# A state-space stage with its channel scales spread first, B and C loaded on two queues, and the first gate panel's units placed between the last read-outs

## The chip, the cores and the metric

One core of a Trainium2 chip runs the whole program. The time is device microseconds of one execution; each kernel is run several times and the median is given. One further execution is taken by the hardware profiler, and all rows of the trace are from that one. The engines are TensorE (PE, its weight loads PEld), VectorE (DVE), ScalarE (ACT), GpSimd (POOL), and SyncE (SP), which issues most transfers.

## The reference

A decoder trunk of two layers over x of 256 steps by 2048 channels, all in float32. A vector c gives six modulation rows per layer (shift, scale and gate for the mixer and for the FFN) by a product with ada_w. Layer 0 mixes with a diagonal state-space model, layer 1 with a convolution; each mixer is followed by a SwiGLU FFN and each sub-layer ends in a LayerNorm. Of layer 0's mixer:

```python
mod = c_act @ ada_w[i] + ada_b[i]            # (2048) x (2048, 6 * 2048), c_act = silu(c)
h = x * (1.0 + sc_m) + sh_m
a_bar = exp(lam * dt)                        # 128 groups of 16 channels, 64 complex states each
b_bar = ((a_bar - 1) / lam) * B              # B: (128, 64, 16) complex, C: (128, 16, 64) complex
state[t] = a_bar * state[t-1] + b_bar @ u[t] # u = h, by groups
y = gelu(real(C @ state) + d_skip * u)
vg = y @ w_glu                               # (256, 2048) x (2048, 4096)
out = vg[:, :2048] * sigmoid(vg[:, 2048:])
```

## The kernel before

**Loads.** A weight "unit" is 512 rows by 512 columns of float32, 1 MB. The modulation of layer 0 is built on PE: 56 units of ada_w (14 blocks of four units, `ada_block`, line 600 on) are multiplied by c_act (line 610), the block's sum is copied to `adas` (ACT, 613), turned (`adat`, 617) and reduced on DVE (`adasum`, 619; `mod`, 620). `ada_units(n)` takes the next n units. They arrive in the `raw` buffers, four at first and six in the loop, all issued by SP in program order, so a load waits for a buffer and everything behind it on SP waits too.

**Preparation.** lam and log_dt are loaded first and turned, and DVE computes exponentials, sines and tables from them (`prep`, lines 67 to 73 of the helper). `load_mats` (210) loads the real and imaginary halves of B and C, C in pieces of 256 bytes so that the two groups of a pair lie together. `turn_mats` (231) turns them on PE (line 240), ACT copies them out (`cm`, 243). `matrices` and `quarter` build the products (`mu`, `qb`, `qc`, line 313) and power tables (`tq`, 351) of four tiles at a time, on DVE for the first four tiles and on POOL for the rest.

**The loop.** 16 tiles of 128 channels. For tile ct: `weights` makes its matrices on ACT and PE (`mb`, `btr`, `lz`; `mc`, `dd`, `bdp`, `bd`); `tables` doubles the table once more (DVE for tile 0, POOL after); `inputs` turns x (`xt`), and ACT scales it with the modulation (`uh`, line 922). The scales have to lie in the states' layout for that: `half_mod` spreads four tiles' scales and shifts with two products (`hmod`, 1268). `drive` gives the states' input (`pin`, 418); `scan` is DVE's recurrence over two half sequences (`x`, `pin`, `pc`, `psn`, lines 435 to 460); `read_out` is the product with C (`y`, 484); `gelu` (1296 to 1306) makes hh and hl, the high and low parts of the next product's input. In turn ct of the loop stand weights, one unit, tables of tile ct+1, the read-out of tile ct-1, inputs, a unit, drive of ct+1, a unit, and then the scan of ct with the gelu of ct-1 between its steps. PE's order is the program's here; the other engines' is the scheduler's, and a call under `queue_behind` or `issue_after` is placed behind the instruction named.

**The gate panels.** w_glu is taken in 8 panels of 512 columns, each of four units, by `gemm` (line 819). For each unit ACT makes `whi` (811) and DVE `wlo` (812), two buffers of each; PE does 24 products (861). The sums `acc` come from a pool of four banks that is opened when the banks of `pin` are given up, so after scan 15. `before` calls `s5_end`, tile 15's read-out and gelu, ahead of unit 2. From panel 1 on an ada queue adds 1.05 steps per unit: a 1 MB load `rawa`, and DVE's sums `adaacc` (678, 680).

Of the kernel before, what the change touches and what calls it, by code (L numbers as in the profile page):

```python
# [153 lines left out]
class S5:  # L154
# [76 lines left out]
    def turn_mats(self):  # L231
        nc, cm = self.nc, self.cm

        for q, n in enumerate(self.nat):
            src = n.rearrange("p (a i) -> p a i", i=GI) if q == 0 else n.rearrange("p (i a) -> p i a", i=GI)
            for h in range(4):
                b = self.bank("turn")
                for i in range(4):
                    one = src[:, :, 4 * h + i] if q == 0 else src[:, 4 * h + i]
                    nc.tensor.transpose(b[:, i * P:(i + 1) * P], one, self.ident)  # L240
# [131 lines left out]
    def weights(self, ct, skip):  # L372

        nc = self.nc
        dd = self.dd[ct % 3]
# [8 lines left out]
        for par in range(2):  # L384
            ps = slice(64 * par, 64 * par + 64)
            nc.scalar.copy(out=mc[ps, 0:4, :, par], in_=qc[ps, :, 4 * k:4 * k + 4])
            nc.scalar.activation(out=mc[ps, 4:6, :, par], in_=qc[ps, 0:3:2, 4 * k:4 * k + 4], func=AF.Copy, scale=-1.0)
# [33 lines left out]
    def scan(self, ct, pin, tab, between):  # L421
# [10 lines left out]
        def turn(out, k):  # L432
            for a in range(2):
                o, i = (z[:, a].rearrange("p s r h c -> p (s r) h c") for z in (out, pin))
                v.tensor_tensor(out=o, in0=i, in1=bc(t[:, k, a::2], 1, 4), op=MUL)  # L435
# [55 lines left out]
def kernel(  # L491
# [311 lines left out]
    class Unit:  # L803


        def __init__(self, wp, wsrc, k0, kn, segs, behind=()):
# [3 lines left out]
            with queue_behind(behind):  # L810
# [450 lines left out]
    def half_mod(q):  # L1261
# [7 lines left out]
        nc.scalar.copy(out=hmod[:, :, :, s4], in_=b[:, 0:16].rearrange("p (h j k) -> p h j k", h=2, j=2))  # L1269

    def inputs(ct):
# [19 lines left out]
    def gelu(ct, u, y):  # L1291
# [10 lines left out]
        def third():  # L1302
            g = w.tile([P, SEQ], F32, tag="gl", name="gl", bufs=1)
            nc.vector.tensor_tensor(out=g.rearrange("p (t c) -> p t c", t=2), in0=uu, in1=vv, op=MUL)
            nc.scalar.copy(out=hh[:, ct], in_=g)
            nc.gpsimd.tensor_tensor(out=hl[:, ct], in0=g, in1=hh[:, ct].bitcast(F32), op=SUB)

# [8 lines left out]
    def start_dense():  # L1316
# [3 lines left out]
        for u in range(2):  # L1320
            ready.append(Unit(wp, s5_w_glu[0], 4 * u, 4, [(0, 256), (D, 256)]))

    const2 = wp = ln_col = wtap = fold32 = row_of = None
    with tc.manual_schedule(engines={mybir.EngineType.PE}):
        ada_units(3)
        for ct in range(-1, NCH):
            now, y = coming, None
# [21 lines left out]
            def between():
                if turns:  # L1350
                    turns.pop(0)()

            if 0 <= ct < NCH:
                held = ct, now[1], *s5.scan(ct, now[2], tabs.pop(ct), between)
                if ct % 4 == 3 and ct < 11:
# [249 lines left out]
```

## Time and profile before

| what | us |
| --- | --- |
| median of 3 runs | 2380.3 (2378.76 to 2382.05) |
| the profiled execution | 2377.07 |
| its span | 2375.3 |
| PE busy | 2276.3 (96% of the span) |
| DVE busy | 1647.3 |
| ACT busy | 1024.6 |
| start of tile 0's scan | 59.57 |
| end of tile 15's scan | 248.90 |

All positions are microseconds from the span's start. A row of the timeline gives start, duration, engine, line of the kernel before, operation, output and inputs, shapes and count, and in square brackets how long the engine stood idle before it and what released it. A row of the windows gives the stretch, its length, the busy time of each engine in it, the granted clock of PE, the busy share of the 16 DMA engines (somewhat over 1 when full) and GB/s. The state-space stage, its preparation included, is the first 250 us; the gate panels end near 440 us, and the rest is FFN, convolution and the second layer, which the change leaves as it is.

### The profile page before, as it was taken

How to read it: one execution, taken by the hardware profiler on the slowest of the kernel's cores; microseconds unless marked ns; L12 is line 12 of the kernel's file. 1: busy time of each engine (PE TensorE's matmuls, PEld its weight loads, DVE VectorE, ACT ScalarE, POOL GpSimd, SP SyncE). 2: the span in 40 equal slices, each digit the busy share in tenths (PEclk: the TensorE clock that was granted, in tenths of full speed). 3: DMA queues.
4: the chain of work that ended last, by engine and by line, in shares of the span. 5: the costliest groups of instructions: out<-in, count | busy, mean ns of one | idle time of the engine just before them, and what ended most of it. 6: DMA issues, size and time to landing. Idle time of an engine off the chain costs nothing.

```text
span 2375.3 us, 34394 instructions
## 1 busy us (share of the span) xinstructions
PE 2276.3 (96%) x14061; PEld 1818.2 (77%) x14061; DVE 1647.3 (69%) x1818; ACT 1024.6 (43%) x1267; POOL 235.3 (10%) x290
## 2 busy tenths in 40 slices
PE   5887899999999999999999999899999999999998
PEld 2444777978888888888886667688888888888888
DVE  6899788887777777777885564788655544554564
ACT  4676234564333333334463332557343333333443
POOL 2564000110000000000031111402000000000000
PEclk7998899999999999999999999999999999999999
DMA  9986599578888888888745553674775555555542
GB/s 309 353 306 207 201 325 344 186 270 304 312 300 314 308 316 297 315 305 316 269 143 177 196 195 125 241 271 161 272 243 178 195 191 181 194 183 191 185 161 98
DMA packets 373332, 572.17 MB, mean 241 GB/s; under 512 B 17171, under 2 KB 267331, under 8 KB 358579
## 3 DMA queue, kind: packets, MB, share of 16 engines
q1 hardware_dynamic: 372742, 569.53, 69.6%
q8 instruction: 110, 1.80, 0.3%
q0 software_dynamic: 192, 0.37, 0.1%
q14 instruction: 48, 0.39, 0.0%
q10 hardware_dynamic: 240, 0.08, 0.0%
HBM read 567.83 MB, written 2.10 MB: 240 GB/s over the span
## 4 chain that ended last, share of the span: by engine, by line
PE 79%; DVE 8%; issue 6%; POOL 4%; ACT 2%; DMA 1%; SPq 0%; DVEq 0%; POOLq 0%; ACTq 0%
PE acc L861 68%; PE acc L865 4%; PE conv L1501 2%; PE turned L877 2%; PE spread L1491 1%; POOL h L959 1%; DVE pin L447 1%; DVE wlo L812 1%; ACT whi L811 1%; DVE pin L435 1%; DVE pc L435 1%; DMA raw<-in_s_w_glu_dram 1%; DVE psn L435 1%; DVE x L435 0%; POOL hf L1540 0%
## 5 line engine op out<-in xcount | busy, mean ns | idle before, releaser
L812 DVE TENSOR_TENSOR wlo<-raw,whi 128x2048 fp32r<-128x2048 f32 x344 | 791.3, 2301 | 544.3 <-ACT whi L811 544.2
L811 ACT CAST whi<-raw 128x2048 fp32r<-128x2048 f32 x344 | 655.0, 1904 | 828.0 <-PE acc L861 613.5
L861 PE MATMUL acc<-whi,h 128*128 128x512 f32 x3648 | 899.4, 396 | 15.6 <-ACT whi L811 8.5
L861 PEld LDWEIGHTS acc<-whi,h 128*128 128x128 f32 x3648 | 680.1, 189 | 175.7 <-issue 17.7
L861 PE MATMUL acc<-wlo,h 128*128 128x512 f32 x1824 | 464.2, 392 | 1.0 <-DVE wlo L812 1.0
L861 PEld LDWEIGHTS acc<-wlo,h 128*128 128x128 f32 x1824 | 342.4, 188 | 77.0 <-DVE wlo L812 1.6
L861 PE MATMUL acc<-whi,f 128*128 128x512 f32 x1248 | 300.5, 391 | 0.0
L680 DVE SCALAR_TENSOR_TENSOR adaacc<-rawa,c_act,adaacc 128x2048 f32<-128x2048 f32 (+1 forms) x135 | 284.7, 2109 | 1.4 <-DMA rawa<-in_ada_w_dram 1.1
L861 PEld LDWEIGHTS acc<-whi,f 128*128 128x128 f32 x1248 | 233.0, 188 | 48.9 <-ACT whi L811 0.8
L861 PE MATMUL acc<-wlo,f 128*128 128x512 f32 x624 | 156.4, 389 | 0.0
L861 PEld LDWEIGHTS acc<-wlo,f 128*128 128x128 f32 x624 | 117.2, 188 | 24.3
L1480 POOL TENSOR_TENSOR lw<-fold,wtap 128x1024 f32<-128x1024 f32 x16 | 41.5, 2601 | 894.2 <-PE acc L865 710.2
L610 PE MATMUL ada<-raw,c_rep 128*32 128x512 f32 x512 | 75.4, 677 | 11.5 <-DMA raw<-in_ada_w_dram 6.7
L959 POOL TENSOR_TENSOR h<-hf,h 128x512 fp32r<-128x512 f32 x24 | 48.2, 2019 | 331.9 <-ACT h L958 324.7
L1184 ACT ACTIVATE fsg<-acc 128x256 f32<-128x256 f32 x84 | 31.9, 380 | 104.3 <-PE acc L861 104.3
L1130 POOL CAST lnmh<-lno 128x2 fp32r<-128x2 f32 x1 | 0.2, 182 | 713.6 <-DVE lno L65 713.6
L865 PEld LDWEIGHTS acc<-h,whi 128*128 128x128 f32 x512 | 63.3, 194 | 9.1 <-DVE h L1530 2.3
L865 PE MATMUL acc<-h,whi 128*128 128x256 f32 x512 | 67.2, 287 | 2.6 <-DVE h L1530 1.4
L1501 PE MATMUL conv<-vs,lw 128*32 128x256 f32 x1024 | 61.4, 381 | 0.4 <-DVE vs L1495 0.4
L1501 PEld LDWEIGHTS conv<-vs,lw 128*32 128x32 f32 x1024 | 33.0, 110 | 25.6 <-issue 4.5
L1185 DVE TENSOR_TENSOR fsg<-acc,fsg 128x256 f32<-128x256 f32 x84 | 35.3, 420 | 19.6 <-ACT fsg L1184 19.5
L447 DVE TENSOR_TENSOR_SCAN pin<-rho,pin 128x256 f32<-128x256 f32 x64 | 44.3, 692 | 1.6
(334 smaller groups left out, 1895.2 us busy)
## 6 DMA issues: line engine op xcount, KB each, us to landing
raw<-in_ffn_w_gu_dram SPq DMA_DIRECT2D x352, 512.0 KB, 4.4
rawa<-in_ada_w_dram SPq DMA_DIRECT2D x128, 1024.0 KB, 5.3
raw<-in_ffn_w_down_dram SPq DMA_DIRECT2D x88, 1024.0 KB, 5.0
raw<-in_ada_w_dram SPq DMA_DIRECT2D x64, 1024.0 KB, 7.4
raw<-in_s_w_glu_dram SPq DMA_DIRECT2D x64, 512.0 KB, 5.4
raw<-in_cv_w_pw_dram SPq DMA_DIRECT2D x64, 512.0 KB, 4.8
raw<-in_cv_w_pw_dram SPq DMA_DIRECT2D x16, 1024.0 KB, 5.7
X<-in_x_dram SPq DMA_DIRECT2D x8, 256.0 KB, 11.0
```

The costliest lines, as they stand in the source:

```text
L435: v.tensor_tensor(out=o, in0=i, in1=bc(t[:, k, a::2], 1, 4), op=MUL)
L447: v.tensor_tensor_scan(out=z, data0=rh[:, a].rearrange("p r h c -> p (r h c)"), data1=z, initial=0.0, op0=MUL, op1=ADD)
L610: nc.tensor.matmul(acc[32 * k:32 * k + 32, :], c_rep[:, 4 * u + k, :], r[:, k, :], start=u == 0, stop=u == 3)
L680: nc.vector.scalar_tensor_tensor(out=acc, in0=r[:, i], scalar=c_act[:, kk:kk + 1], in1=acc, op0=MUL, op1=ADD)
L811: m1 = nc.scalar.copy(out=self.hi[:, :kn], in_=r[:, :kn])
L812: m2 = nc.vector.tensor_tensor(out=self.lo[:, :kn], in0=r[:, :kn], in1=self.hi[:, :kn].bitcast(F32), op=SUB)
L861: nc.tensor.matmul(acc[bank].rearrange("p a b -> p (a b)"), x[:, bank * HALF:(bank + 1) * HALF], wt[:, k], start=first, stop=end)
L865: nc.tensor.matmul(acc[bank][:, i], wt[:, k, m * P:(m + 1) * P], x, start=first and i == 0, stop=end and i == 1)
L877: nc.tensor.transpose(b[:, o:o + HALF], u[t][:, c0 + k * P:c0 + (k + 1) * P], ident)
L959: nc.gpsimd.tensor_tensor(out=hl[:, s2], in0=h, in1=hh[:, s2].bitcast(F32), op=SUB)
L1480: nc.gpsimd.tensor_tensor(out=lw, in0=fold32.unsqueeze(1).unsqueeze(1).broadcast_to([P, 4, CONV_G, 32]), in1=bc(wtap[:, :, 4 * ch:4 * ch + ...
L1501: nc.tensor.matmul(acc[32 * q:32 * q + 32, :], lw[:, q, g, :], vs[:, q, 4 * g:4 * g + SEQ], start=g == 0, stop=g == CONV_G - 1)
```

## The change

1. `load_mats` makes four contiguous loads of 512 KB instead of two and four; the real halves are issued by SP, the imaginary halves by ACT, as ACT's first and third transfers. C then lies with the pair's groups apart, and `turn_mats` turns it with two products of 64 columns in place of one transpose.
2. `half_mod(0)`, the spreading of the first four tiles' scales, stands ahead of the loop and no longer in `inputs(0)`. The three units ahead of the loop are gone, every turn has three units, the last one too.
3. `weights` is cut in two. `weights_in` (mb, btr, lz) stays where it was; `weights_out` (dd, mc, bdp, bd) comes after `drive`. Its copies of mc are placed behind the first hmod copy. Units follow each of weights_in, inputs and weights_out.
4. The loop ends one turn sooner. Only one unit of w_glu is made ready ahead. The first gate panel gets its sums in one bank of the pool `aux` (three banks, used for y, adat, xt and others) and in the bank of `ada`; `before` becomes a table: ahead of unit 1 `last_scan` (read-out 14 and scan 15), ahead of unit 2 a mark, ahead of unit 3 `s5_end`. Unit 3 of that panel is taken by its four row blocks in turn instead of by banks.
5. `held_back`: from unit 3's casts on, whi and wlo are placed behind scan 15's last instruction, and after `s5_end` the casts and the ada steps of panel 0's rest and of panel 1 behind tile 15's gelu.

```diff
     def load_mats(self, b_re, b_im, c_re, c_im):
         nc = self.nc
-        for r, t in enumerate((b_re, b_im)):
-            nc.sync.dma_start(self.nat[0][64 * r:64 * r + 64], t.rearrange("(j a) n i -> j (a n i)", a=2))
-        for r, t in enumerate((c_re, c_im)):
-            for a in range(2):
-                nc.sync.dma_start(
-                    self.nat[1][64 * r:64 * r + 64].rearrange("p (i a n) -> p i a n", i=GI, a=2)[:, :, a],
-                    t.rearrange("(j a) i n -> j a i n", a=2)[:, a])
+        for q, parts in enumerate(((b_re, b_im), (c_re, c_im))):
+            for r, (t, eng) in enumerate(zip(parts, (nc.sync, nc.scalar))):
+                eng.dma_start(self.nat[q][64 * r:64 * r + 64], t.rearrange("(j a) x y -> j (a x y)", a=2))
...
-                    one = src[:, :, 4 * h + i] if q == 0 else src[:, 4 * h + i]
-                    nc.tensor.transpose(b[:, i * P:(i + 1) * P], one, self.ident)
+                    for a in range(2):
+                        nc.tensor.matmul(b[64 * a:64 * a + 64, k], src[:, a, 4 * h + i], self.ident, start=True, stop=True)
...
+    def weights_out(self, ct, skip, behind):
+        nc.scalar.mul(dd, self.ident, skip)
+        with self.tc.issue_after(behind.ins):
...
-            with queue_behind(behind):
+            with queue_behind([*behind, *held_back]):
                 m1 = nc.scalar.copy(out=self.hi[:, :kn], in_=r[:, :kn])
...
-            if u == 2 and before:
-                before()
-            for part in ((0,), (1,)) if last else ((0, 1),):
+            if u in before:
+                before[u]()
+            for part in ((0,), (1,)) if last and not in_turn else ((0, 1),):
...
+                if last and in_turn:
+                    order.sort(key=lambda o: o[1])
...
-        for u in range(2):
-            ready.append(Unit(wp, s5_w_glu[0], 4 * u, 4, [(0, 256), (D, 256)]))
+        ready.append(Unit(wp, s5_w_glu[0], 0, 4, [(0, 256), (D, 256)]))
...
-        ada_units(3)
-        for ct in range(-1, NCH):
+        first_mod = half_mod(0)
+        for ct in range(-1, NCH - 1):
...
+            s5.weights_in(ct + 1)
+            ada_units(1)
...
+            u, uh = inputs(ct + 1)
+            ada_units(1)
+            coming = ct + 1, u, s5.drive(ct + 1, uh)
+            s5.weights_out(ct + 1, d_col[:, ct + 1:ct + 2], first_mod)
+            ada_units(1)
...
+    def last_scan():
+        ada_turn()
+        scan(NCH - 1, coming, s5.read_out(*held))
+        pin_ctx.close()
+        accp = ctx.enter_context(tc.tile_pool(name="acc", bufs=4, space=PSUM))
...
+        first = {"acc": [b.rearrange("p (a b) -> p a b", b=SEQ) for b in (aux("acc"), bank)], "before": {1: last_scan, 2: lambda: held_back.append(s5.end), 3: s5_end}}
```

PE around tile 0, from the last units ahead of the loop to the first pin. Before (ada is one unit for every four products; adat is a block's turn, hmod the spread scales):

```order
L610 MATMUL ada<-raw,c_rep 32x512 x12
L393 MATMUL btr<-ident,mb_478 128x128 x4
L396 MATMUL bdp<-fold,dd_488 128x32
L400 MATMUL bdp<-mc_480,mb_478 32x32 x8
L610 MATMUL ada<-raw,c_rep 32x512 x4
L1276 MATMUL xt<-ident,X 128x128 x2
L1280 MATMUL xt<-ident,X 32x128 x8
L617 MATMUL adat<-ident,adas 128x128 x4
L1268 MATMUL hmod<-mod_128,sel 128x8 x2
L610 MATMUL ada<-raw,c_rep 32x512 x4
L418 MATMUL pin<-uh,lz_483 128x2x64 x8
```

The same place now, where the first row is units 6 to 8 of the program (another twelve products that stood ahead of the piece shown before):

```order
L615 MATMUL ada<-raw,c_rep 32x512 x12
L622 MATMUL adat<-ident,adas 128x128 x4
L1276 MATMUL hmod<-mod_128,sel 128x8 x2
L386 MATMUL btr<-ident,mb_492 128x128 x4
L615 MATMUL ada<-raw,c_rep 32x512 x4
L1284 MATMUL xt<-ident,X 128x128 x2
L1288 MATMUL xt<-ident,X 32x128 x8
L615 MATMUL ada<-raw,c_rep 32x512 x4
L423 MATMUL pin<-uh,lz_497 128x2x64 x8
```

Three units fewer stand ahead of pin (10 instead of 13), hmod ahead of the tile's own products, and bdp behind pin.

PE at the end of the stage, from tile 15's pin on. Before (y are the read-outs of tile 14 and then of tile 15, acc the first gate panel, 24 products a unit):

```order
L418 MATMUL pin<-uh,lz_484 128x2x64 x8
L473 MATMUL y<-u,bd_487 128x129
L474 MATMUL y<-u,dd_490 128x128
L484 MATMUL y<-pc,mc_482 32x128 x16
L484 MATMUL y<-psn,mc_482 32x128 x16
L861 MATMUL acc<-whi,h 128x512 x16
L861 MATMUL acc<-wlo,h 128x512 x8
L861 MATMUL acc<-whi,h 128x512 x16
L861 MATMUL acc<-wlo,h 128x512 x8
L473 MATMUL y<-u,bd_485 128x129
```

Now, from the last unit of ada on (bd_501 is tile 14's, bd_499 tile 15's):

```order
L615 MATMUL ada<-raw,c_rep 32x512 x4
L870 MATMUL acc<-whi,h 128x512 x16
L870 MATMUL acc<-wlo,h 128x512 x8
L622 MATMUL adat<-ident,adas 128x128 x4
L478 MATMUL y<-u,bd_501 128x129
L479 MATMUL y<-u,dd_504 128x128
L489 MATMUL y<-pc,mc_496 32x128 x16
L489 MATMUL y<-psn,mc_496 32x128 x16
L870 MATMUL acc<-whi,h 128x512 x16
L870 MATMUL acc<-wlo,h 128x512 x8
L870 MATMUL acc<-whi,h 128x512 x16
L870 MATMUL acc<-wlo,h 128x512 x8
```

Unit 0 stands ahead of read-out 14, units 1 and 2 between the read-outs, and unit 3 behind tile 15's, where units 0 and 1 stood between them and 2 and 3 behind.

DVE where scans 14 and 15 overlap (tab_2826 and tab_2792 are tile 14's, tab_2969 and tab_2950 tile 15's). Before:

```order
L812 TENSOR_TENSOR wlo<-raw,whi 128x2048
L454 TENSOR_TENSOR cx<-pin,rw 128x8
L455 TENSOR_TENSOR cy<-pin,rw 128x8
L812 TENSOR_TENSOR wlo<-raw,whi 128x2048
L457 TENSOR_TENSOR cx<-cx,cy 128x2x2
L458 TENSOR_TENSOR cx<-cx,cy 128x2x2
L435 TENSOR_TENSOR x_3128<-pin,tab_2969 128x512
```

Now:

```order
L817 TENSOR_TENSOR wlo<-raw,whi 128x2048
L440 TENSOR_TENSOR pc<-pin,tab_2792 128x512 x2
L440 TENSOR_TENSOR psn<-pin,tab_2792 128x512 x2
L817 TENSOR_TENSOR wlo<-raw,whi 128x2048
L624 TENSOR_REDUCE adasum<-adat 128x4
L440 TENSOR_TENSOR pin<-pin,tab_2950 128x512
L625 SCALAR_TENSOR_TENSOR mod_128<-adasum,adab_120 128x4
L817 TENSOR_TENSOR wlo<-raw,whi 128x2048
L440 TENSOR_TENSOR pin<-pin,tab_2950 128x512
```

Three wlo instead of two stand ahead of scan 15's main part, the last two behind scan 14's end; the two adaacc that stood within scan 15 are behind tile 15's gelu.

On ACT, ahead of tile 0's uh, there stand now two tab copies, an activation and a copy of mc; on POOL the loads of ln_g and ln_b, which wait for PE's vec_t, have moved ahead of the clears of mb, mc, bd and rho; on ACT near the end whi of units 3 and 4 stand ahead of the gelu of tile 15.

More of the change, by code (lines that the diff above doesn't have):

```diff
@@ L394, in weights @@
         nc.scalar.copy(out=self.lz[ct % 2].rearrange("p h r b -> p (h r b)"), in_=bb)
+    def weights_out(self, ct, skip, behind):
+        nc, k = self.nc, ct % 4
+        qc, mb, mc = self.qm[ct // 4][1], self.mb[ct % 2], self.mc[ct % 3]
+        dd = self.dd[ct % 3]
+        nc.scalar.mul(dd, self.ident, skip)
+        with self.tc.issue_after(behind.ins):
+            for par in range(2):
+                ps = slice(64 * par, 64 * par + 64)
+                nc.scalar.copy(out=mc[ps, 0:4, :, par], in_=qc[ps, :, 4 * k:4 * k + 4])
+                nc.scalar.activation(out=mc[ps, 4:6, :, par], in_=qc[ps, 0:3:2, 4 * k:4 * k + 4], func=AF.Copy, scale=-1.0)
         bk = self.bank("bdp")
@@ L813, in __init__, with gemm @@
             self.marks = [m1, m2]
-    ready = []
-    def gemm(wsrc, k0, kch, segs, x2, wp, feed=None, ahead=None, banks=((0, 1), (2, 3)), before=None, wide=True):
-        acc = [accp.tile([P, 2, SEQ], F32, tag="acc", name="acc") for _ in range(2)]
+    ready, held_back = [], []
+    def gemm(wsrc, k0, kch, segs, x2, wp, feed=None, ahead=None, banks=((0, 1), (2, 3)), before={}, acc=None, wide=True):
+        in_turn = acc is not None
+        acc = acc or [accp.tile([P, 2, SEQ], F32, tag="acc", name="acc") for _ in range(2)]
         units = list(range(0, kch, 4))
@@ L1319, in start_dense, with scan, between @@
         wp = mctx.enter_context(tc.tile_pool(name="w", bufs=2, reuse_waits="tile"))
-        for u in range(2):
-            ready.append(Unit(wp, s5_w_glu[0], 4 * u, 4, [(0, 256), (D, 256)]))
+        ready.append(Unit(wp, s5_w_glu[0], 0, 4, [(0, 256), (D, 256)]))
     const2 = wp = ln_col = wtap = fold32 = row_of = None
+    def scan(ct, now, y):
+        nonlocal held
+        turns = list(gelu(*held[:2], y)) if held else []
+        def between():
+            if turns:
+                turns.pop(0)()
+        held = ct, now[1], *s5.scan(ct, now[2], tabs.pop(ct), between)
+        while turns:
+            between()
@@ L1349, in between @@
[L1349 to L1355, printed above, removed]
-                    extra = s5.matrices(ct // 4 + 2, nc.gpsimd)
-                with queue_behind([s5.last]):
-                    next(extra, None)
-                    if ct % 4 == 1 and ct < 12:
-                        s5.quarter(ct // 4 + 1, nc.gpsimd)
@@ L1361 @@
-            while turns:
-                between()
-    pin_ctx.close()
-    accp = ctx.enter_context(tc.tile_pool(name="acc", bufs=4, space=PSUM))
+            u, uh = inputs(ct + 1)
[3 more added lines that the diff above has]
+            ada_units(1)
+            if ct == NCH - 2:
+                raws[:] = [rawp]
+                more.close()
+                s5.keep_ctx.close()
+                start_dense()
@@ new lines @@
+            if ct < 0:
+                continue
+            scan(ct, now, y)
+            if ct % 4 == 3 and ct < 11:
+                extra = s5.matrices(ct // 4 + 2, nc.gpsimd)
+            with queue_behind([s5.last]):
+                next(extra, None)
+                if ct % 4 == 1 and ct < 12:
+                    s5.quarter(ct // 4 + 1, nc.gpsimd)
+    accp = None
+    def last_scan():
+        nonlocal accp
+        ada_turn()
+        scan(NCH - 1, coming, s5.read_out(*held))
+        pin_ctx.close()
+        accp = ctx.enter_context(tc.tile_pool(name="acc", bufs=4, space=PSUM))
@@ L1419 @@
         stats = Stats("ln00", sp)
-        for k in range(12):
-            later.put(5 + k, lambda: ada_units(1))
         def enter(name, stats, i, k, raw, pairs):
@@ L1435 @@
         f0ctx = ExitStack()
+        bank = auxp.tile([P, 512], F32, tag="ada", name="acc", bufs=1)
+        first = {"acc": [b.rearrange("p (a b) -> p a b", b=SEQ) for b in (aux("acc"), bank)], "before": {1: last_scan, 2: lambda: held_back.append(s5.end), 3: s5_end}}
         for i in range(8):
```

59 lines of the change are left out of this document (22 added, 37 removed).

## The prediction

> **What bounds the kernel now.** I read the page first (PE 96% busy over the span, so only the stretches in which PE is not the bound can give much), then the windows of the first 300 us, the timeline of each engine there, and the waits of DVE. Only two places before the dense stages have PE idle: the start, and the end of the state-space stage.
>
> The start. Rows of the windows: window, length, busy PE, PEld, DVE, ACT, POOL (instructions), granted clock, DMA share, GB/s.
>
> ```profile
> 10.00:15.00 5.00, 4.28 (x24) 0.70 (x24) 4.83 (x26) 0.00 (x0) 0.00 (x0) 1.00 1.05 378
> 15.00:20.00 5.00, 2.32 (x12) 0.20 (x8) 5.00 (x19) 0.00 (x0) 0.00 (x0) 0.78 1.08 266
> 20.00:25.00 5.00, 2.54 (x16) 2.54 (x13) 5.00 (x29) 1.96 (x5) 0.00 (x0) 0.50 1.25 170
> ...
> 25.00:30.00 5.00, 2.10 (x11) 1.73 (x10) 5.00 (x38) 3.43 (x10) 0.20 (x1) 0.50 1.19 248
> 81.50:97.50 16.00, 10.69 (x130) 6.15 (x130) 11.24 (x24) 7.94 (x24) 11.42 (x19) 0.75 1.06 375
> 110.00:121.00 11.00, 9.01 (x156) 5.55 (x152) 10.55 (x22) 8.19 (x26) 5.91 (x11) 1.00 0.99 355
> ```
>
> The DMA engines are full until 97 us (share over 1), but while C moves they carry only 170 to 266 GB/s instead of 378. DVE is full from 15 us on, and full again in the loop (10.55 of 11 us in the last row); between the two it stands empty. What it waits for is in the timeline of the same stretch (start, duration, engine, line) and in DVE's waits (total, times, longest):
>
> ```profile
> 2.01 2.07 DMA lam<-in_s_lam_im_dram
> 29.04 1.08 PE L240 MATMUL turn<-ident,nat 128*128 128x128 f32 x4 [2.90 <-DMA nat<-in_s_c_im_dram]
> 41.87 0.41 ACT L360 COPY tab<-tq 128x256 f32<-128x256 f32 x1
> 42.67 0.42 DVE L351 TENSOR_TENSOR xt<-tab,wt 128x256 f32<-128x256 f32 x1
> 43.46 0.49 DVE L351 TENSOR_TENSOR tab<-xt,yt 128x128 f32<-128x128 f32 x2
> 44.56 0.30 ACT L387 ACTIVATE mc<-qc 64x128 f32<-64x128 f32 x1
> 44.88 0.40 ACT L386 COPY mc<-qc 64x256 f32<-64x256 f32 x1
> 57.36 1.06 PE L610 MATMUL ada<-raw,c_rep 128*32 128x512 f32 x8
> 57.67 0.81 ACT L922 ACTIVATE uh<-xt,hmod 128x128 f32<-128x128 f32 x2
> 58.36 1.16 PE L418 MATMUL pin<-uh,lz 64*128 64x128 f32 x16
> 59.57 1.29 DVE L435 TENSOR_TENSOR x<-pin,tab 128x512 f32<-128x512 f32 x2 [2.07 <-PE pin L418]
> ```
>
> ```profile
> DVE adasum L619 <- PE adat L617: 12.8, 2, 7.9
> DVE vec L532 <- PE vec_t L530: 0.8, 1, 0.8
> ...
> DVE u L1299 <- ACT u L1296: 7.6, 6, 4.3
> ```
>
> DVE has its tables at 43.95, but tile 0's scan starts at 59.57: PE must first have taken 13 units of 1 MB, in program order, ahead of pin. That is 13 + 2 (B, C) + 1 (two X quarters) = 16 MB, and a full stream brings no more by then. From 59 to 222 us DVE is the bound: its longest wait there is the last row, 7.6 us over 15 tiles. So whatever tile 0 gains is carried to the end of the loop.
>
> The end. The timeline from scan 13's last product on (the three psn rows end scans 13, 14 and 15):
>
> ```profile
> 220.93 1.28 DVE L435 TENSOR_TENSOR psn<-pin,tab 128x512 f32<-128x512 f32 x2
> 231.30 2.28 DVE L812 TENSOR_TENSOR wlo<-raw,whi 128x2048 fp32r<-128x2048 f32 x1
> 238.64 1.28 DVE L435 TENSOR_TENSOR psn<-pin,tab 128x512 f32<-128x512 f32 x2
> 240.43 0.75 DVE L678 TENSOR_SCALAR adaacc<-rawa,c_act 128x1024 f32<-128x1024 f32 x1
> 241.69 1.26 DVE L680 SCALAR_TENSOR_TENSOR adaacc<-rawa,c_act,adaacc 128x1024 f32<-128x1024 f32 x1
> 242.46 0.39 ACT L1296 ACTIVATE u<-y 128x256 f32<-128x256 f32 x1 [12.39 <-PE y L484]
> 245.36 0.72 POOL L1306 TENSOR_TENSOR h<-gl,h 128x256 fp32r<-128x256 f32 x1 [11.34 <-ACT h L1305]
> 247.62 1.28 DVE L435 TENSOR_TENSOR psn<-pin,tab 128x512 f32<-128x512 f32 x2
> 249.05 5.89 PE L861 MATMUL acc<-whi,h 128*128 128x512 f32 x16 [6.64 <-DVE psn L435]
> 256.60 3.83 PE L861 MATMUL acc<-whi,h 128*128 128x512 f32 x16
> 263.54 1.06 PE L484 MATMUL y<-psn,mc 128*32 128x128 f32 x32
> 264.52 3.95 PE L861 MATMUL acc<-whi,h 128*128 128x512 f32 x16
> 275.64 0.60 PE L617 MATMUL adat<-ident,adas 128*128 128x128 f32 x4
> 275.99 3.93 PE L861 MATMUL acc<-whi,h 128*128 128x512 f32 x16
> ```
>
> The first gate panel does not start before scan 15's last product (DVE, 248.90), since its sums lie in the banks of pin. All four units then run alone, the first at a low clock (16 matmuls in 5.89 instead of 3.83 us), with the read-out of tile 15 between, and the panel ends at 275.64: 26.7 us after scan 15, 53.4 after scan 13 (222.21).
>
> **The change, part by part.**
>
> *B and C in four contiguous loads.* Three 5-us windows lost 3 x 378 - (266 + 170 + 248) = 450 GB/s x 5 us = 2.2 MB, which is 6 us at 378. On PE, 32 narrow products replace 16 transposes for C: 4 transposes took 1.08, so 16 take 4.3, and 32 take between half of that and 8.6; I take 5. They lie before 33 us, when PE still waits for units 5 to 7, and so cost nothing; uncovered they would cost 4.
>
> *Two queues.* ScalarE issues both imaginary halves, 1 MB, as its first transfers, beside lam, on which the whole DVE preparation hangs. lam landed in 2.07 us on an empty stream. The delay lies between 0 and the whole megabyte at 378 GB/s, 2.8 us; I take 2, nearer the upper end, since the halves are queued no later than lam.
>
> By the Trainium skill (DMA: Bandwidth & Descriptors, Issuing engines are not separate DMA queues) transfers from different engines share the same 16 DMA engines, so a second queue adds no rate; Queues, rings and completion order adds that each engine goes round-robin between queues by packets. By that rule alone lam loses about its wait for alternate packets, the upper part of the span, and the sum for the start would be 1 us poorer than mine; no run here shows two loaded queues yet.
>
> *Scales ahead of tile 0.* PE now needs 10 units, not 13, before pin, and one X quarter: 10 + 2 + 0.5 = 12.5 MB, from 4 us on (lam lands at 4.08) at 378 GB/s: landed at about 37 us. Then DVE and ACT decide. DVE's work to 43.95 has 1.0 us of waits in it (vec 0.8, mu 0.2) and 1.28 of tables (42.67 to 43.95), so the quarter tables end at 41.7; 0.3 for one adasum pair moved ahead, 2 for lam: 44.0. ACT then has in its row, ahead of uh, two tab copies, an activation and a copy of mc and uh itself: 0.41 + 0.41 + 0.30 + 0.40 + 0.81 = 2.3, with 0.2 for hand-overs 46.5. From uh's end (58.48) to the scan (59.57) it was 1.1. So the scan of tile 0 starts at 47.6: **12 us gained**. Without lam's delay 14; if PE at half clock (0.50 in the rows) doubles the 4 us of hmod, btr, xt, two units and pin ahead of the scan, 8. POOL's two ln loads now stand ahead of its clears of mb, mc, bd and rho and wait for vec_t; the clears must be in by 44 us for ACT, and vec_t follows C's turn at about 30, so that is covered by some 8 us.
>
> *Weights in two halves, one unit after each.* In the loop PE's order changes, its instructions do not; DVE is the bound there, and pin of the next tile is needed only when the scan under way ends. Taken as 0, between -2 and +3.
>
> *Panel units between the last read-outs.* On DVE three wlo (2.28 each) now stand ahead of scan 15's end instead of two, and the adaacc pair (0.75 and 1.26, some 1.9 with overlap) is held behind gelu 15: 26.7 + 2.3 - 1.9 + 0.3 (adasum) = 27.4 after scan 13, plus a wait: wlo of unit 2 needs a whi that is free only when PE has finished unit 0, and all of scan 15 is queued behind it. I price that at 1 (0 to 3): scan 15 ends at 28.4. PE: unit 0 can start when its casts are through, about 9.5 us after scan 13 (the wlo row above begins 9.1 after it), takes 5.6 (264.52 to 275.64 is two units) to 7.6 at the low clock, then read-out 14 (2.4: unit 1 from 256.60 with 5.6, end at 264.60), units 1 and 2, read-out 15 and unit 3: 9.5 + 6.5 + 2.4 + 11.2 + 2.4 + 5.6 = 37.6, with adat 38. Gelu of tile 15 (242.46 to 246.08 for tile 14: 3.6) hides behind unit 3's first three chunks (three quarters of 5.6, 4.2). On ACT the whi of units 3 and 4 stand before u of tile 15; unit 4's needs unit 2 done, which PE also needs before read-out 15, so it costs nothing unless it slips by a cast (1.9). **53.4 - 38 = 15 us gained**, 12 to 18.
>
> *What is late next.* The gate panels carry raw and rawa 1:1:
>
> ```profile
> 251.44 0.92 SPq L567 DMA_DIRECT2D raw<-in_s_w_glu_dram  x2
> 397.91 0.34 SPq L665 DMA_DIRECT2D rawa<-in_ada_w_dram  x1
> 402.26 11.78 SPq L567 DMA_DIRECT2D raw<-in_s_w_glu_dram  x10
> 274.23 1.28 DVE L680 SCALAR_TENSOR_TENSOR adaacc<-rawa,c_act,adaacc 128x1024 f32<-128x1024 f32 x1
> 276.00:304.00 28.00, 28.00 (x126) 22.90 (x124) 24.62 (x26) 10.92 (x11) 0.00 (x0) 1.00 0.80 275
> 388.00:416.00 28.00, 27.53 (x123) 21.05 (x122) 23.92 (x16) 11.58 (x10) 0.00 (x0) 1.00 1.04 358
> ```
>
> Before, four steps of adaacc (eight instructions, 240.43 the first and 274.23 the last) were done by 276; now none is when panel 1 starts: 4 MB (11 us at 358 GB/s) and 10 us of DVE move into panels 1 to 6, where DMA has its slack in the early windows (0.80) and DVE is idle some 4 of 28 us. That fits on average, but each raw then lands just in time. I take 2 us given back, 0 to 6.
>
> **Sum.** -12 - 15 + 0 + 2 = -25. The profiled execution has 2377.07 us (span 2375.3), 3.2 below the median of the runs shown, 2380.3; so 2352 against the profile, and **2355** on the scale of the medians.
>
> **Rivals.** *The stream still decides the start* (0.12): DMA is full to 97 us in before; if X or the later units come no sooner than C's saving, only 6 of the 12 us come: 2361. For it: share 1.05; against it: three units fewer are needed. *The fill does not fill* (0.08; this is the change not doing what it says): the casts of units 1 and 2 wait for PE and scan 15 stands behind them, so that it ends some 8 to 10 us later: 15 becomes 6, 2364. Against it: PE and ACT had sat idle there (6.64 us before acc, 12.39 before u). *The gate panels become bound by DMA and DVE* (0.08): 10 of the 25 are given back, 2365. *Slower* (0.03): the same stream to its end. From 251.44 to about 419 (414.0 and some 5 to land), 27 raw and 22 rawa units, 49 MB, ran at 292 GB/s. It now begins some 20 us sooner, at 232. If waits for the four buffers held it to 49 MB in 187 us, 262 GB/s, the panels would end no sooner than now; at 250 the stage would be 9 us longer, 2389. The lowest window of it above ran at 275, so this needs a rate not seen there.
>
> **Numbers.** My forecast has 0.69. The range takes the sums of the ends: -14 - 18 - 2 + 0 = -34 would be 2346, and -8 - 12 + 3 + 6 = -11 gives 2369; both ends at once is unlikely, so 2345 to 2368, which holds the first three rivals' times too. A measurement of this kernel tells about 0.2% (4.8 us) from no change. Faster by more than that 0.93, within it 0.04 (most of what is gained given back), slower 0.03.
>
> **What would show it.** Right: x of tile 0 near 47 us, DMA at 370 GB/s through 15 to 30 us, DVE without the 12.8 us for adasum; PE busy with acc before scan 15's last psn, the first 16 of panel 1 some 9 to 11 us after it; the last panels' PE rows full. Wrong: tile 0 still behind ada units of PE; wlo of unit 2 preceded by some microseconds of idle DVE; whi waiting for raw with PE idle in panels 1 to 6.

## The result and the profile after

The changed kernel takes 2364.8 us (median of four executions, 2361.0 to 2369.5), the kernel before beside it 2380.2 (2378.8 to 2382.1): a ratio of 0.9936, 95% interval 0.9917 to 0.9955. The profiled execution took 2360.99 (span 2359.0), 16.1 less than the profiled one of before. The gain forecast was 25.

The span is cut here at the same four events in every profile: the start of tile 0's scan (first `x<-pin`), the end of scan 13's last `psn`, the first `turned` of the gate panels (in panel 1), and the first product of panel 7 (`acc<-h,whi`). The five stretches add up to the span. All kernels of the study stand in the table, the ratios with their intervals. Line numbers in rows are those of the kernel that was profiled: the changed kernel's L440 is L435 of the kernel before.

| kernel | ratio to before | to tile 0 | loop to scan 13 | end, to panel 1 | panels to 7 | rest |
| --- | --- | --- | --- | --- | --- | --- |
| before | 1 | 59.6 | 162.6 | 59.4 | 136.2 | 1957.5 |
| changed | 0.9936 (0.9917 to 0.9955) | 51.7 | 165.0 | 44.8 | 140.5 | 1957.0 |
| e0, changed again | 0.9937 (0.9919 to 0.9955) | 58.7 | 167.3 | 43.4 | 140.6 | 1956.8 |
| e1, one queue | 0.9944 (0.9929 to 0.9959) | 52.0 | 165.0 | 44.8 | 142.2 | 1962.3 |
| e2, behind lam | 0.9950 (0.9935 to 0.9964) | 56.9 | 169.9 | 44.6 | 140.0 | 1958.0 |
| e3, start only | 1.0002 (0.9988 to 1.0016) | 51.4 | 164.9 | 60.9 | 137.1 | 1957.2 |
| e4, end only | 0.9945 (0.9930 to 0.9960) | 59.4 | 162.1 | 42.0 | 143.1 | 1958.3 |
| e5, 16 MB left out | one run, 2363.1 us | 53.1 | 169.8 | 44.6 | 132.9 | 1960.9 |
| e6, units in the loop | 0.9979 (0.9970 to 0.9989) | 50.5 | 178.4 | 51.6 | 132.9 | 1958.1 |
| e7, weights together | 0.9943 (0.9926 to 0.9959) | 51.9 | 166.8 | 42.1 | 144.1 | 1955.0 |
| f1, clears behind | 0.9943 (0.9929 to 0.9957) | 55.9 | 164.5 | 44.8 | 143.2 | 1957.5 |
| f3, tile 0 first | 0.9915 (0.9901 to 0.9928) | 47.9 | 169.2 | 43.1 | 141.7 | 1959.2 |
| f4, same, two queues | 0.9924 (0.9912 to 0.9937) | 49.9 | 168.7 | 43.6 | 140.3 | 1957.0 |
| f5, units later | 0.9932 (0.9918 to 0.9945) | 46.8 | 168.3 | 44.1 | 140.4 | 1959.8 |

The rest is code that the change doesn't touch, and it took 1955.0 to 1962.3 from one profile to the next: a difference of under some 5 us between two single profiles says something only by the stretch in which it arises.

The windows of the changed kernel's start (columns as before):

```profile
5.00:10.00 5.00, 1.38 (x4) 0.72 (x4) 0.53 (x2) 0.00 (x0) 0.00 (x0) 1.00 1.01 252
...
15.00:20.00 5.00, 3.71 (x20) 0.24 (x12) 5.00 (x24) 0.00 (x0) 0.00 (x0) 1.00 1.08 376
20.00:25.00 5.00, 2.87 (x13) 1.16 (x14) 5.00 (x18) 0.59 (x1) 0.00 (x0) 1.00 1.02 197
```

The dip of the rate has moved, not gone: it lies where the imaginary halves move (252) and where the real ones do (197). DVE's waits up to tile 0:

```profile
DVE lt L224 <- PE lamt L222: 5.8, 1, 5.8
DVE adasum L624 <- PE adat L622: 2.2, 1, 2.2
DVE xt L351 <- ACT tab L360: 2.0, 1, 2.0
DVE x L440 <- PE pin L423: 2.0, 1, 2.0
```

The 12.8 us for adasum are down to 2.2. lt, the turned lam from which DVE's preparation starts, stands 4.3 us later than before (9.29, before 5.00). PE and DVE ahead of tile 0's scan:

```profile
44.43 0.99 PE L1276 MATMUL hmod<-mod,sel 128*128 128x8 f32 x4 [1.18 <-DVE mod L625]
45.27 1.09 PE L386 MATMUL btr<-ident,mb 128*128 128x128 f32 x4
46.30 1.94 PE L615 MATMUL ada<-raw,c_rep 128*32 128x512 f32 x8
48.16 0.69 PE L1284 MATMUL xt<-ident,X 128*128 128x128 f32 x2
48.78 0.89 PE L1288 MATMUL xt<-ident,X 128*32 128x128 f32 x16
49.50 1.03 PE L615 MATMUL ada<-raw,c_rep 128*32 128x512 f32 x8
50.46 1.16 PE L423 MATMUL pin<-uh,lz 64*128 64x128 f32 x16
51.67 1.29 DVE L440 TENSOR_TENSOR x<-pin,tab 128x512 f32<-128x512 f32 x2 [2.01 <-PE pin L423]
```

From hmod to the scan PE stands in one row without a gap, with two units between; the first takes 1.94 us, the second 1.03, and the granted clock from 45 to 52 us is 0.69. The end, from scan 13's last product to panel 1:

```profile
215.99 0.68 DVE L440 TENSOR_TENSOR psn<-pin,tab 128x512 f32<-128x512 f32 x1
...
226.75 5.30 PE L870 MATMUL acc<-whi,h 128*128 128x512 f32 x15 [0.75 <-ACT adas L618]
244.82 1.28 DVE L440 TENSOR_TENSOR psn<-pin,tab 128x512 f32<-128x512 f32 x2
255.97 3.82 PE L870 MATMUL acc<-whi,h 128*128 128x512 f32 x16
```

Scan 15 ends 29.4 us after scan 13 (216.67), and panel 1 begins 39.3 after it, before 53.8. The gate panels, as windows and, over panels 1 to 6, as groups (busy, mean ns, idle time before them); of the groups the rows of the changed kernel come first, then those of the kernel before:

```profile
256.00:276.00 20.00, 20.00 (x91) 16.39 (x90) 19.64 (x20) 7.17 (x7) 0.00 (x0) 1.00 0.91 315
276.00:304.00 28.00, 26.97 (x116) 20.86 (x115) 23.40 (x22) 10.51 (x9) 0.00 (x0) 1.00 1.00 351
```

```profile
L870 PE MATMUL acc<-whi,h 128*128 128x512 f32 x384 | 94.9, 397 | 2.1 <-ACT whi L816 1.8
...
L816 ACT CAST whi<-raw 128x2048 fp32r<-128x2048 f32 x25 | 47.6, 1905 | 54.6 <-DMA raw<-in_s_w_glu_dram 50.0 <-PE acc L870 4.7
...
L861 PE MATMUL acc<-whi,h 128*128 128x512 f32 x384 | 94.7, 396 | 0.6 <-ACT whi L811 0.4
...
L811 ACT CAST whi<-raw 128x2048 fp32r<-128x2048 f32 x25 | 47.6, 1905 | 56.3 <-DMA raw<-in_s_w_glu_dram 36.0 <-PE acc L861 14.4 <-PE turned L877 5.8
```

The stream is full (share 1.00, before 0.80 in this window), and of whi's 54.6 us of waiting 50.0 are for raw, before 36.0 of 56.3. PE itself stands idle 2.4 us in panels 1 to 6, before 0.6.

### The profile page after: what moved, and what is told of

Its sections match the earlier page's. It is cut to its first block, busy times and chain, and to the rows that moved or that the text cites. A ratio compares the mean times of both kernels' runs of the same rounds, so it can differ in the third digit from the quotient of the medians.

```text
span 2359.0 us, 34477 instructions
## 1 busy us (share of the span) xinstructions
PE 2278.7 (97%) x14109; PEld 1817.0 (77%) x14109; DVE 1647.2 (70%) x1818; ACT 1024.3 (43%) x1267; POOL 235.8 (10%) x290
## 4 chain that ended last, share of the span: by engine, by line
PE 78%; DVE 8%; issue 6%; POOL 3%; ACT 3%; DMA 2%; ACTq 0%; DVEq 0%; SPq 0%; POOLq 0%
PE acc L870 66%; PE acc L874 4%; PE conv L1523 2%; PE turned L886 2%; DMA raw<-in_s_w_glu_dram 1%; PE spread L1513 1%; DVE wlo L817 1%; ACT whi L816 1%; POOL h L968 1%; DVE pin L452 1%; PE y L489 1%; DMA nat<-in_s_b_re_dram 1%; DVE adaacc L685 1%; DVE x L440 0%; DVE pin L440 0%
```

## The experiments

**e0: the changed kernel again.** 

> The changed kernel once more, as the base for the runs beside it. Both theories: ratio 0.992 to 0.995 to the kernel before, x of tile 0 at 51 to 52 us, scan 13 to panel 1's first matmul 38 us, panels 1 to 6 145 to 147 us. If x of tile 0 or the loop differs by over 1 us from the first profile, differences of that size between kernels say nothing.

Four executions: 2360.4, 2361.1, 2367.4, 2368.6. The slowest was profiled, and its tile 0 starts at 58.7, almost as late as before the change. DVE in it, then POOL:

```profile
35.73 4.83 DVE L65 TENSOR_SCALAR wt<-wt 128x64 f32<-128x64 f32 x1
35.83 4.73 DVE L73 SCALAR_TENSOR_TENSOR wt<-wt 128x64 f32<-128x64 f32 x1
40.59 0.36 DVE L70 TENSOR_TENSOR rw<-wt,par 128x64 f32<-128x64 f32 x2
```

```profile
35.57 0.52 POOL L528 DMA_DIRECT2D ln_r<-in_ln_b_dram  x1
36.08 0.54 POOL L195 MEMSET mb<- 128x512 f32 x1
...
40.28 0.22 POOL L195 MEMSET bd<- 128x128 f32 x1
```

In the first profile the same operations of DVE end ahead of POOL's:

```profile
34.05 0.20 DVE L65 TENSOR_SCALAR wt<-wt 128x64 f32<-128x64 f32 x1
34.15 0.23 DVE L73 SCALAR_TENSOR_TENSOR wt<-wt 128x64 f32<-128x64 f32 x1
```

A 0.20 us operation takes 4.83: it ends 0.06 us after the last of POOL's ten clears. It belongs to the last scalar operations of the preparation; in the first profile they were 1.7 us earlier and done at 34.4, ahead of the first clear (35.71). The 1.7 us are DVE's wait for adat, which now stands within the preparation: 3.86 us here, 2.21 in the first profile. The Trainium skill (SBUF — State Buffer, Who interferes with whom) says that DVE's two-port modes, which a tensor_scalar can enter, and GpSimd lock each other out of a shared port, the later one being blocked entirely. The trace agrees as far as the two exclude each other, and shows that a row of clears without gaps isn't broken into; in which mode the operation ran no row shows, and by the recorded starts it stood still from 0.35 us ahead of the first clear on, which isn't explained. The kernel before has a smaller case, where two clears in a row end at 7.77 and DVE's operation at 7.82:

```profile
5.97 1.85 DVE L67 TENSOR_SCALAR ops<-ops 128x64 f32<-128x64 f32 x1
7.01 0.76 POOL L195 MEMSET mc<- 128x768 f32 x1
```

Since tile 0 differs by 7.0 us between two profiles of one kernel, and the loop by 2.3, such differences between kernels count below only where the rows that make them can be read.

**e1: one queue.**

```diff
-            for r, (t, eng) in enumerate(zip(parts, (nc.sync, nc.scalar))):
+            for r, (t, eng) in enumerate(zip(parts, (nc.sync, nc.sync))):
```

> The imaginary halves go back to SyncE's queue behind the four ada loads; the contiguous loads stay. Theory A (lam sharing the stream with 1 MB sets the start): lt near 5.0 us instead of 9.3, the DVE preparation 4 us earlier, x of tile 0 at 47.5 to 49 instead of 51.7, the whole 2 to 4 us faster than the changed kernel. Rival B (the order on ScalarE and the ada units set tile 0, lam's delay is covered): lt at 5.0 as well, but x of tile 0 stays within 1 us of 51.7 and the time too. Rival C (the halves in one row take the stream's rate down longer): B turns after 26 us and x of tile 0 is later than 52.

lt is back at 5.02, and DVE's preparation is 4 us earlier, but tile 0 starts at 52.0. DVE's longest wait:

```profile
DVE x L440 <- PE pin L423: 7.7, 1, 7.7
```

Rival B holds: DVE now waits for PE, whose row from hmod (44.40) to pin is the same as above but for 0.4 us. lam's delay was covered; theory A falls. Of the whole nothing was gained: the four executions lie from 2363.3 to 2368.2, and in the profiled one, in which no operation of DVE stands still after 8 us, the rest took 1962.3. So e0's collision isn't all that spreads the times.

**e2: halves behind lam.** All four halves are issued behind a copy on ScalarE that reads lt; this moves ScalarE's two, as SyncE's stand behind four units anyway.

```diff
+        self.lam_in = nc.scalar.copy(out=pp.tile([P, 1], F32, name="lam_in"), in_=lt[:, 0, 0:1])
...
+                with self.tc.issue_after(self.lam_in.ins):
```

> The imaginary halves stay on ScalarE's queue, but are issued there behind a copy that reads lt, so that lam has the stream to itself and the halves of B come side by side. Theory A: lt near 5.0, x of tile 0 at 47.5 to 49, 2 to 4 us faster than the changed kernel. Theory D (a transfer into 64 partitions moves at about 200 to 250 GB/s, and two halves of 64 side by side run at the full 375): windows between 10 and 25 us all over 330 GB/s, B turned before 20 us, x of tile 0 a further 1 us earlier than in the one-queue run. Rival E (the rate falls for these 8 KB rows however they are queued): the dip to some 200 GB/s remains for about 10 us in all. Rival B: x of tile 0 within 1 us of 51.7.

```profile
10.00:15.00 5.00, 1.45 (x8) 0.00 (x0) 4.79 (x27) 0.00 (x0) 0.00 (x0) 1.00 1.04 215
15.00:20.00 5.00, 1.93 (x8) 0.20 (x8) 5.00 (x20) 0.00 (x0) 0.00 (x0) 1.00 1.02 277
20.00:25.00 5.00, 1.94 (x8) 0.20 (x8) 3.74 (x17) 0.00 (x0) 0.00 (x0) 1.00 1.08 300
25.00:30.00 5.00, 4.27 (x19) 2.57 (x20) 0.00 (x0) 1.80 (x4) 0.00 (x0) 1.00 0.99 261
```

Side by side the halves move no faster: 215 to 300 GB/s over 20 us. Theory D falls, E holds, and tile 0 starts at 56.9; DVE waits 9.4 us for adat in its preparation. The four windows carried 5.3 MB, of which the halves are at most 2.1, so other loads run in them too. The Trainium skill (SBUF — State Buffer, Door 1: The DMA port swizzle) has 196 GB/s for 64 partitions, since they reach half of the ports. The Trainium skill (SBUF — State Buffer, "Can I just issue two DMAs to hit both halves?") has only 6% more for two such transfers at once. The 197 of the changed kernel and the 215 here lie near these; a transfer of the same bytes into all 128 partitions wasn't tried, so the cause isn't shown.

**e3 and e4: one part alone.** e3 has the new start and loop with the old end; e4 the old loads, scales and loop with the new end.

```diff
 e3
...
-        first = {"acc": [b.rearrange("p (a b) -> p a b", b=SEQ) for b in (aux("acc"), bank)], "before": {1: last_scan, 2: lambda: held_back.append(s5.end), 3: s5_end}}
+        first = {"before": {2: s5_end}}
...
 e4
...
-        first_mod = half_mod(0)
+        ada_units(3)
```

> The new start and the new order in the loop, with the old end: scan 15 ahead of all gate units, four sums in the old banks, two units cast ahead. Terms of the profile of the changed kernel: start -7.9, loop +3.5, end 0, gate panels 0: some 4 us faster than the kernel before, 2376. If the loop's loss was chance of one profile, 8 us faster, 2372. If the start alone is given back in the gate panels (the stream sets them): 0 to 2 us faster.

> The old start, loads and loop order with the new end (panel units between the last read-outs, sums in free banks, steps held back). Terms of the profile of the changed kernel: scan 13 to panel 1 38 us instead of 53.8 (-15.7), panels 1 to 6 +4: 11.5 us faster than the kernel before, 2368.7. If the give-back in the gate panels needs the earlier start as well: -15, 2365. If the loop's loss belongs to the end part (units of the last tiles) it shows here: -8, 2372.

The end alone has nearly all of the gain (0.9945), the start alone none in the median (1.0002). e3's ten executions reach from 2373.0 to 2388.2; the profiled one (2373.5) is among the fastest, and its start and loop are those of the first profile (the stretches against before: -8.2, +2.3, +1.5, +0.9, -0.3, together -3.8). None of the slower ones was profiled, so where they lose the rest is open. In e4 the end is 17.4 shorter and the panels are 6.9 longer: the give-back comes without the earlier start too.

**e5 and e6: what sets the gate panels.**

```diff
 e5
...
-    ada = AdaQueue([(0, 3, 2), (0, 4, 0), (0, 5, 0)] + [(1, j, 0) for j in range(5)] + [(1, 5, 2)])
+    ada = AdaQueue([(0, 3, 2), (0, 5, 0)] + [(1, j, 0) for j in range(5)] + [(1, 5, 2)])
-            ada.rate = 1.05
+            ada.rate = 0.35
...
 e6
-    parts = [(j, q) for q in range(4) for j in (0, 1)] + [(2, q) for q in range(4)] + [(3, 0), (3, 1)]
+    parts = [(j, q) for q in range(4) for j in (0, 1)] + [(2, q) for q in range(4)] + [(3, q) for q in range(4)]
...
-            ada_units(1)
+            ada_units(1 + (ct + 1 >= 8))
...
-            ada.rate = 1.05
+            ada.rate = 0.8
```

> Leaves out one of the six modulation rows of the first layer (index 4, taken as zero), 16 of the 24 MB of rawa that the gate panels carry, with the rate of the steps lowered to a third, so that the 8 that stay are spread; DVE loses about 40 us of work there. Theory F (panels 1 to 6 are now set by the DMA stream, each raw landing just in time): their 146.0 us fall to the PE's own 141 to 142, idle of PE before acc under 0.5 us, no whi behind a raw with PE idle. Rival G (the order of turns, read-outs and adar on PE sets it): 144 to 146 us as now.

> Eight more ada units (8 MB) go into the loop, one a tile from tile 8 on, by PE, where the stream has slack, and eight DVE steps fewer into the gate panels (rate 0.8 instead of 1.05). Theory F: panels 1 to 6 go from 146 to 141.5 to 143; the loop pays 8 x 1.04 us on PE, hidden as long as DVE is the bound there, and two adasum pairs (0.8) on DVE: the whole 2 to 4 us faster than the changed kernel. Rival H (PE or the stream has no room in tiles 8 to 15): the loop grows by 3 to 8 us and the whole is the same or slower.

Window and group of e5:

```profile
276.00:304.00 28.00, 28.00 (x125) 22.84 (x124) 20.46 (x22) 11.46 (x9) 0.00 (x0) 1.00 0.79 258
```

```profile
L871 PE MATMUL acc<-whi,h 128*128 128x512 f32 x384 | 93.9, 394 | 0.0
```

Without 16 of the 24 MB no PE time is lost, whi waits for no raw, and the panels take 132.9 instead of 140.5. Theory F's mechanism holds: PE's 2.4 us of waiting are gone. The other 5.2 us are not waiting: 2.7 are PE's own work that left with the row (adar from 3.2 to 1.1, adat from 1.1 to 0.5), the rest is products that take a little less each. The run takes DVE's work away together with the loads; that the stream and not DVE was late is read from whi's 50.0 us for raw.

e6 gets the same 132.9 by moving 8 MB (adar is 1.1 there too), and pays 13.4 in the loop and 6.8 in the end. So the loop grows, as rival H has it, by more than its 3 to 8, and for units that are 8.3 us on PE. That PE or the stream has no room in tiles 8 to 15, H's reason, isn't shown: from 180 to 210 us PE is busy some 85% and the stream's share is under 0.9, while from 150 us on DVE waits 8.0 us for ScalarE's part of the gelu and 4.8 for adat.

**e7: weights together.**

```diff
             s5.weights_in(ct + 1)
+            if ct >= 0:
+                s5.weights_out(ct + 1, d_col[:, ct + 1:ct + 2], first_mod)
             ada_units(1)
...
```

> The two halves of a tile's weights stand together again ahead of its first unit, for tiles 1 to 15; all else is the changed kernel. Theory I (the loop's 3.5 us come from splitting the weights): from x of tile 0 to scan 13's last product 162.6 us as before the change, instead of 166.2, and the whole 3 us faster than the changed kernel. Rival J (they come from elsewhere, the units' places, or an earlier start that meets the stream): 165 to 167 us, and the whole within 1 us of the changed kernel.

166.8: theory I falls, rival J holds.

**f1: clears behind the preparation.**

```diff
+        done = nc.gpsimd.tensor_copy(out=w.tile([P, 2], F32, name="done"), in_=self.rw[:, :, 0])
...
+                    with self.tc.issue_after(done.ins):
```

> GpSimd's ten clears of mb, mc, bd and rho wait for the last of DVE's prep (rw), by a small copy that reads it; all else is the changed kernel. Theory K (DVE's small scalar operations stand still while GpSimd clears, 4.7 us in one, where the clears fall before the end of prep, which 0.1 to 2 us of DMA time decide): no wt operation over 0.3 us in the profile, x of tile 0 at 51.5 to 53 in every execution, and the runs within about 5 us of one another around 2361 to 2363, with none near 2368. Rival L (the two groups of times, near 2361 and near 2368, come from elsewhere, the clock or the gate panels): still both groups, spread 7 to 9 us, mean 2364.

Five executions: 2363.0, and four from 2367.3 to 2368.1. No operation of DVE stands still, but POOL's does; POOL, then DVE:

```profile
35.96 5.22 POOL L192 COPY done<-rw 128x2 f32<-128x2 f32 x1
41.12 0.52 POOL L197 MEMSET mb<- 128x512 f32 x1
...
45.31 0.20 POOL L197 MEMSET bd<- 128x128 f32 x1
```

```profile
34.53 0.34 DVE L70 TENSOR_TENSOR rw<-wt,par 128x64 f32<-128x64 f32 x2
...
41.08 0.20 DVE L539 COPY vec<-vec_t 128x64 f32<-128x64 f32 x1
```

The copy of two elements a partition begins inside an unbroken row of DVE's two-input products, and ends when DVE comes to a copy: a lock of the same kind, the other way round. The clears behind it, which read nothing, run beside the next products of DVE in their usual 0.52. They are 5 us later, ScalarE's mb, rho and adas copies behind them, and tile 0 at 55.9. So theory K's forecast of the times failed, while its mechanism shows from the other side; a kernel that takes only the collision away was not had, and between K and L the run doesn't decide. In f4, with the same edit, POOL got in first:

```profile
35.96 0.32 POOL L192 COPY done<-rw 128x2 f32<-128x2 f32 x1 [0.28 <-DVE rw L70]
```

**f3 and f4: tile 0 first on PE.** Ahead of pin stand btr and xt, then the scales; the three units follow drive. f3 has e1's queue, f4 two queues and f1's clears.

```diff
-        if ct % 4 == 0 and ct:
-            half_mod(ct // 4)
+        first = half_mod(ct // 4) if ct % 4 == 0 else None
...
-            ada_units(1)
+            ada_units(ct >= 0)
...
+            ada_units(1 if ct >= 0 else 3)
```

> One queue for B and C as in the one-queue run, and on PE tile 0's btr and xt ahead of the scales, its three ada units behind its pin. Theory M (with lam early, tile 0 waits for the chain from the last unit of the scales: adas, adat, hmod, then two units and xt at half clock, uh, pin): x of tile 0 at 47 to 48.5 instead of 52.0 in the one-queue run; 3 to 4 us earlier at scan 13, and the whole at 2358 to 2361 if the gate panels keep half of it or more. Theory N (the gate panels, at the rate of their stream, take back what the start gains): x of tile 0 as said, but the whole stays within 1.5 us of the one-queue run, 2364 to 2367.

> The same order of tile 0 on PE, with the imaginary halves back on ScalarE's queue as in the changed kernel, and the clears behind rw. If lam's delay of 4.3 us counts once PE's order is out of the way: x of tile 0 at 49 to 51, 2 us or more behind the run with one queue. If it does not: x within 1 us of that run. The time by theory M 2359 to 2363, by theory N 2363 to 2366.

f3's tile 0 starts at 47.9, as theory M has it, and f4's 2.0 later, where lt comes at 10.60. In f4 the scan follows DVE's last table without a wait, so with PE's row out of the way lam seems to count (the clears differ too):

```profile
49.45 0.49 DVE L353 TENSOR_TENSOR tab<-xt,yt 128x128 f32<-128x128 f32 x2
49.87 1.28 DVE L442 TENSOR_TENSOR x<-pin,tab 128x512 f32<-128x512 f32 x2
```

But f3's tile 1 ends at 75.6 instead of 73.4 us, since its pin stands behind five units; DVE's two waits for pin, of tiles 0 and 1:

```profile
DVE x L440 <- PE pin L423: 7.4, 2, 4.0
```

f3 is the fastest of all, 2359.5 (2357.4 to 2362.9); its interval meets that of the changed kernel. The time is where theory M has it, but not by M's way: scan 13 ends at 217.1, as in e1, so what the start gained is gone by then.

**f5: two units later still.** f3 with one unit behind tile 0's pin and two behind tile 3's.

```diff
-            ada_units(1 if ct >= 0 else 3)
+            ada_units(3 if ct == 2 else 1)
```

> The run with tile 0 first on PE, but of tile 0's three units only one stands behind its pin; the two others go behind tile 3's pin, into the 16 us of tile 2, where DVE waits for GpSimd's products by way of ScalarE and PE has room. Theory M (each link of the start is kept if no later one takes it back; in the run before it was tile 1, whose pin stood behind five units): x of tile 0 at 48, tile 1 done near 69.5 instead of 75.6, tile 2 at 84 to 87 instead of 90.0, scan 13 at 211 to 214 instead of 217.1, the whole 2354 to 2358, no group of times 7 us higher. Theory N' (the stream holds the loop: units and X arrive no sooner): PE waits for raw ahead of pin in tiles 1 to 4, scan 13 at 216 to 218, 2359 to 2361. Theory N (the gate panels take it back): scan 13 early, but panel 7 no earlier than 400 us.

Tile 0 at 46.8, tile 1 done at 68.6, tile 2 at 85.3, as theory M has it; but scan 13 at 215.1, later than its 211 to 214, panel 7 at 399.6, 2.4 earlier than in the changed kernel, and the median 2362.4, above its 2358 and no better than f3's. In tile 2 what waits is now this (ScalarE, for POOL's products of the next four tiles):

```profile
ACT mc L399 <- POOL qc L313: 7.6, 1, 7.6
```

In the changed kernel this wait was 2.7. Of 4.9 us gained at tile 0, 1.6 are left at scan 13: the loop is no plain sum of DVE's work. Over it DVE's waits for ScalarE's part of the gelu sum to 13.1 us, in the changed kernel to 7.0; what makes ScalarE late in tiles 3 to 13 isn't settled.

## Why the prediction was right in sign and 10 us off in size

*The start, -12 (-8 to -14): it was -7.9 in one execution and -0.9 in another.* Two steps failed. First, the forecast of 47.6 took the time from uh to the scan over from before, and left PE's row, doubled at half clock, to the bad end of the range. From hmod to the scan it is 7.2 us here; where two units, btr and xt no longer stand between them, 3.8 (f3) and 4.3 (f4). That is 3.0 to 3.4 of the 4.1 us missed. That f3's 47.9 lies so near the step's 47.6 is partly luck, since lam isn't late in f3 and the step had added 2 us for it. Second, "the clears must be in by 44 us for ACT ... covered by some 8 us" looked for who waits for the clears, not for whom they disturb. Moved behind the wait for vec_t, they met the end of DVE's preparation; 1.7 us of DVE's row decide over 4.7. That this is behind the two groups of times in e0 is shown for the two profiled executions only.

*Two queues, 2 of the start:* 4.3 in size, 0 in effect (e1), and up to 2.0 where PE's row doesn't hide it (f4). The estimate's upper end, 2.8, was the whole megabyte at 378 GB/s; the window in which it moved had 252, and at that rate a megabyte is 4.2 us. Why the rate is so low when the halves move is not shown (e2). *Contiguous loads, 6 us of the stream:* below 378 in the windows 5 to 10 and 20 to 25 us lie (126 + 181) x 5 us = 1.5 MB, 4 us; so 2 were saved. The dip had been put down to C's short pieces, though B's contiguous halves, turned from 22.5 on, must have moved in the window of 15 to 20 (266).

*The loop, 0 (-2 to +3): +2.4, and +4.7 in e0.* It comes with the new order: with the old one the loop takes 162.6 and 162.1 (e4), in every profile with the new one 164.5 or more, also where tile 0 starts late (e0) and where the weights stand together (e7). On DVE it can be read in part. Its waits in this stretch sum to 10.2 us, before 8.7, those for adat alone to 2.1, before 0.3. And the two small sums of each tile take 9.2 us, before 6.9. Of the first of the two, these are the rows for tiles 5 to 13, before and after:

```profile
L457 DVE TENSOR_TENSOR cx<-cx,cy 128x4 f32<-128x4 f32 x9 | 1.7, 194 | 0.2
```

```profile
L462 DVE TENSOR_TENSOR cx<-cx,cy 128x4 f32<-128x4 f32 x9 | 2.9, 318 | 0.2
```

The long ones fall beside POOL's products: the one at 119.85 takes 0.68 us and ends with POOL's qc, one with POOL idle 0.16. Why the new order brings them together is open. The reading that "whatever tile 0 gains is carried to the end of the loop" doesn't hold: of 7.9 us 5.5 are left at scan 13, in f5 7.1 of 12.8.

*The end, -15 (12 to 18): -14.6, -16.0 in e0, -17.4 in e4.* Right, step by step: scan 15 at 29.4 after scan 13 (28.4 forecast), panel 1 at 39.3 (38). The rival by which the fill doesn't fill falls.

*The gate panels, +2 (0 to 6): +4.3.* The mechanism was named, as "each raw then lands just in time". From panel 1's first product on it is +4.2 (146.0, before 141.8). Of that 1.8 are PE's waits, so the named mechanism was priced about right in this profile (in e4 PE's waits are 4.2). What the term lacked is PE's own work: 1.1 for a set of adar products that is now taken in two parts, at 1.04 us each instead of 1.05 for both; the rest isn't read. It had been added on average rates, but the windows from 276 to 388 have the stream at shares of 0.93 to 1.02. Of the rivals this one came nearest, at 4 of its 10 us. The others fall: ahead of tile 0 it is PE's own row that ends last, not the stream (f3, with e1's loads, starts 4 us sooner than e1), and at 340 GB/s over panels 1 to 6 the stream is far from the 262 of the slower case.

In sum -7.9 + 2.4 - 14.6 + 4.3 - 0.5 = -16.3 for the span of the first profile, and -0.9 + 4.7 - 16.0 + 4.4 - 0.7 = -8.5 for that of e0, against -25. The range's lower end, 2345, lies just below the 2346 that its own sum of the ends gives.

## What to carry to other kernels

When an operation moves on an engine that can lock another out, ask not only who waits for it but what it will run beside: here ten clears cost DVE 4.7 us in one profile and nothing in another. An earlier start is worth only what the next engine's row leaves of it; price that row at the clock that the trace shows there (here a unit took 1.94 us instead of 1.03). And when leaving work out shortens a stretch, first subtract the work itself: of e5's 7.6 us only 2.4 were waiting. Where four executions fall into two groups, profile one of each before believing a single profile.

## What was not expected of the hardware

A DVE operation of 0.20 us took 4.83 beside a row of POOL clears, and a POOL copy of two elements a partition 5.22 beside a row of DVE's two-input products: each waits for the whole row, not for one instruction of it. Where the contiguous halves move, loads into 64 partitions, the lowest 5 us window has 195 to 230 GB/s in each profile, however the halves were queued; windows without them, from 5 to 45 us, have 340 to 388. And lam, two transfers of 32 KB, was used 4.3 us later beside 1 MB on another engine's queue.
